# Differential attention of a hybrid decoder step: prompt scores of both components in two halves of the array's rows, component weights on GpSimd, a prompt step within the sample softmax, turned weights in other banks

## The chip, the cores and the metric

The kernel runs on one core of a Trainium2 chip. The engines are TensorE (PE: matmuls and transposes into PSUM; PEld are its weight loads), VectorE (DVE), ScalarE (ACT), GpSimd (POOL) and SyncE (SP, which issues most DMAs). The metric is the device time of one launch in microseconds (us), the median of several runs.

## The reference

One layer of a decoder serves a prompt of 512 rows and a sample group of 8 sequences of 4 rows with the same weights. The part that matters here is differential attention: 4 heads, each with two 64-wide components of q and k and a 128-wide v.

```python
def diff_attend(q, k, v, mask, lam):
    s = jnp.einsum('bqhcd,bkhcd->bhcqk', q.astype(jnp.float32), k.astype(jnp.float32)) * (DA_QK_DIM ** -0.5)
    s = jnp.where(mask[None, None, None], s, -jnp.inf)
    p = jax.nn.softmax(s, axis=-1)
    a = p[:, :, 0] - lam * p[:, :, 1]
    return jnp.einsum('bhqk,bkhd->bqhd', a, v.astype(jnp.float32))
```

The prompt is done in 4 blocks of 128 query rows; block b sees 128(b+1) keys. The sample rows see 256 cached keys and 4 new ones. Around it stand an mLSTM head group, an output projection, cross-attention into 256 memory tokens and a gated FFN with a short convolution.

## The kernel before

The program is one straight stream of about 17,000 instructions. A framework schedules it: the code emits operations, and the framework's own timing model decides the order in which each engine issues them, each engine then working through its own list in order. Python generators set what is emitted near what. Float32 matmuls run in two passes, so one `mm` of float32 operands is two rows of the trace; the matmuls of weights have operands split into high and low parts of a rounded float32 type and run in one pass each.

The stage that the change touches runs from about 246 to 302 us of the span. Two things are interleaved in it:

- **The prompt**: 16 groups i (block b = i // 4, head h = i % 4), run by `pipe(4 * H, da_soft, idle, da_turn, da_av, da_end)`. One `next(prompt)` is a step: it emits the scores and the softmax of group i, the transposes of group i - 2, the product with v of group i - 3, and after a block's last head its norm. `da_soft` takes two score banks `sda`, one for each component, from the pool `mm` (5 PSUM banks), multiplies 128 queries with 128(b+1) keys for each component, adds the causal mask to the last 128 columns by a bf16 matmul with the identity, takes row maxima on DVE, exponentials and row sums `su` on ACT, then the weights `rc` (reciprocals of the two sums, the second times the first sum and -lambda) and joins the components with them in `pda` on DVE. `da_turn` transposes `pda` into a bank `tpa`, ACT copies it to `aT`; `da_av` multiplies it with `dvN`.
- **The samples**: for each of 8 sequences `dk_load`, `dk_turn` (transposes `tpk` of cached keys) and `dk_scores` (`ssc`, four heads in four column quarters of the array). `sample_softmax` then makes weights `csz`, combines the components (`spa`), copies them (`spc`), transposes them (`spt`) and spreads them over `az`. Then come the products with the cached v (`ops`, four column quarters). In the first loop `next(prompt)` runs once per turn, ten times; the next five run beside the loads of v.

Both components of q lie in one tile `dqT` (and of k in `dkT`), component 0 in partitions 0 to 63, component 1 in 64 to 127. To multiply one component alone, the kernel keeps a second tile `dqz` with the lower half zeroed (four ACT copies and a POOL memset) and zeroes the upper half of `dqT` (four POOL memsets). Each score matmul so contracts over all 128 rows of the array, half of them zeros.

The pool `at` has 3 PSUM banks and serves transposes and small results (`tpk`, `mlt`, `dat`, `spa`, `spt`, `ops`). Tiles with the tag `S` share 11 buffers in SBUF; `dqz` takes one. Weights of the next projection (`w_out`) are loaded to staging buffers that the cached v occupies until `ops` has used it. After the stage the output projection runs, with the last groups' transposes and products among its matmuls.

Of the kernel before, what the change touches and what calls it, by code (L numbers as in the profile page):

```python
# [7 lines left out]
F32 = mybir.dt.float32  # L8
# [4 lines left out]
ALU = mybir.AluOpType  # L13
AX = mybir.AxisListType

P = 128
DM = 1024
SEQ = 512
NB = 8
# [3 lines left out]
H = 4  # L23
# [54 lines left out]
def kernel(ctx: ExitStack, tc: tile.TileContext, I, O):  # L78
    nc = tc.nc
    MUL, ADD, SUB, MAX, MIN = ALU.mult, ALU.add, ALU.subtract, ALU.max, ALU.min  # L80
# [9 lines left out]
    cst = ctx.enter_context(tc.tile_pool(name="cst", bufs=1))  # L90
# [11 lines left out]
    def S(shape, dt, name):  # L102
        return sp.tile(list(shape), dt, name=name, tag="S")
# [10 lines left out]
    def at(name="at"):  # L114
        return psa.tile([P, 512], F32, name=name, tag="at")

    def mmp(name="mm"):
        return psm.tile([P, 512], F32, name=name, tag="mm")
# [11 lines left out]
    mm = nc.tensor.matmul  # L130
# [24 lines left out]
    def con(n, p=P):  # L155
        o, w = CONST_COLS[n]
        return cpk[:p, o:o + w]
# [182 lines left out]
    @contextmanager  # L340
    def burst(ins):

        if ins is None:
            yield
        else:
            with tc.issue_after(ins), tc.high_priority():
                yield
# [687 lines left out]
        VRED(out=nm[:, b:b + 1], in_=ps, axis=AX.X, op=MAX, negate=True)  # L1035
        ACT(out=sall[:, b, :], in_=ps, func=AF.Exp, bias=nm[:, b:b + 1], accum_out=su[:, b:b + 1])

    def sample_softmax(sall, su, coef, sel, oname):


        cf = small(NB, "scf")
        nc.vector.reciprocal(out=cf, in_=su)
        if coef is not None:
            VTS(out=cf, in0=cf, scalar1=coef, scalar2=None, op0=MUL)
        VTT(out=cf, in0=cf, in1=sel, op=MUL)
        VTT(out=view(csz, 0, [(64, NB // 2), (48, 2), (1, 16)]),
            in0=con("comb").unsqueeze(1).unsqueeze(1).broadcast_to([P, NB // 2, 2, 16]),
            in1=cf.rearrange("p (i e) -> p i e", e=2).unsqueeze(3).broadcast_to([P, NB // 2, 2, 16]), op=MUL)
        az = S([P, 2, H, NB * NS], F32, oname + "z")
        nc.gpsimd.memset(az, 0.0)  # L1050
        w = sall.shape[2]
        pa = at("spa")
        for e in range(2):
            for i in range(NB // 2):
                mm(pa[NS * i:NS * i + NS, :w], lhsT=csz[:, 2 * i + e, :], rhs=sall[:, 2 * i + e, :], start=(e == 0), stop=(e == 1))
        a = Z("spc")[:, :w]
        nc.scalar.copy(out=a, in_=pa[:, :w])
        pT = at("spt")
        for g in range(2):
            tr(pT[:, g * P:(g + 1) * P], a[:, g * P:(g + 1) * P], ident)  # L1060
        for g in range(2):
            src = pT[:, g * 128:(g + 1) * 128].rearrange("p (b h t) -> p h b t", b=NB, h=H)
            for h in range(H):
                nc.scalar.copy(out=view(az, g * 1024 + h * 256, [(36, NB), (1, TS)]), in_=src[:, h])
        return a, [az[:, 0], az[:, 1]]
# [100 lines left out]
        rr = slice(64 * c, 64 * c + 64)  # L1166
        nc.gpsimd.tensor_copy(out=qz[rr, :, :, c, :], in_=dqT[rr, :, SEQ:].rearrange("p h (g r) -> p h g r", g=2))


    dqz = S([P, H, SEQ], F32, "dqz")  # L1170
    nc.gpsimd.memset(dqz[0:64], 0.0)
    for b in range(4):
        c = slice(b * P, b * P + P)
        nc.scalar.copy(out=dqz[64:128, :, c], in_=dqT[64:128, :, c])
        nc.gpsimd.memset(dqT[64:128, :, c], 0.0)

    kst, kts, pts, aTs, outs, rcs = {}, {}, {}, {}, {}, {}

    def dk_load(b):
# [22 lines left out]
    def da_soft(i):  # L1202
        b, h = i // H, i % H
        c0 = b * P
        nk = c0 + P
        pt = pts[i] = N("pda").rearrange("p (c k) -> p c k", c=2)
        nm = small(2, "nm")
        su = small(2, "su")
        sv = [mmp("sda")[:, :nk] for _ in range(2)]
        for c in range(2):  # L1210
            mm(sv[c], lhsT=(dqz if c else dqT)[:, h, c0:c0 + P], rhs=dkT[:, h, 0:nk], start=True, stop=False)
            mm(sv[c][:, c0:nk], lhsT=identb, rhs=cmaskb, start=False, stop=True)
        for c in range(2):
            VRED(out=nm[:, c:c + 1], in_=sv[c], axis=AX.X, op=MAX, negate=True)
            ACT(out=pt[:, c, :nk], in_=sv[c], func=AF.Exp, bias=nm[:, c:c + 1], accum_out=su[:, c:c + 1])
        rc = sm.tile([P, 2], F32, name="rc", tag="rc", bufs=6)
        nc.vector.reciprocal(out=rc, in_=su)
        VTS(out=rc[:, 1:2], in0=rc[:, 1:2], scalar1=su[:, 0:1], scalar2=nlam, op0=MUL, op1=MUL)
        STT(out=pt[:, 0, :nk], in0=pt[:, 1, :nk], scalar=rc[:, 1:2], in1=pt[:, 0, :nk], op0=MUL, op1=ADD)
        rcs[i] = rc  # L1220

    def da_turn(i):
        b = i // H
        nk = (b + 1) * P
        tp = mmp("tpa")
        for j in range(b + 1):
            tr(tp[:, j * P:(j + 1) * P], pts[i][:, 0, j * P:(j + 1) * P], ident)
        aTs[i] = Z("aT")
        nc.scalar.copy(out=aTs[i][:, :nk], in_=tp[:, :nk])
# [22 lines left out]
    for t, _ in enumerate(pipe(NB, dk_load, dk_turn, dk_scores)):  # L1252
        if t == 3:
            F.add(out_gate())
        F.run(2.5)
        next(prompt)
        F.run(2.5)
    aw, az = sample_softmax(sall, su, cv, con("selD"), "da")
    F.run(4)
    pz = Z("pz")[:, :NS]  # L1260
    VTT(out=v2(pz, TS), in0=aw[:, 256:260].unsqueeze(1).broadcast_to([P, NB, TS]),
# [616 lines left out]
```

## Time and profile before

| | |
|---|---|
| median of 3 runs | 960.0 us (959.2 to 962.14) |
| the profiled execution's own time | 957.37 us |
| its span | 955.6 us |
| instructions | 17087 |
| DVE busy | 600.3 us (63%) |
| ACT busy | 387.7 us (41%) |
| POOL busy | 196.4 us (21%) |
| PEclk | 0.9 or more in all slices but the last |

The span is the time from the first to the last instruction of the profiled execution; what lies around it is 957.37 - 955.6 = 1.8 us. A row of the timeline gives a start, a duration, the engine, the line, the operation, what it writes and reads and how many rows were merged; in square brackets stands the idle time before it and who ended it. Durations of matmuls are modelled and overlap, so what a matmul costs is read from the starts of neighbouring rows.

### The profile page before, as it was taken

Reading aid. Unit: us, or ns where it says so; the run is one execution under the profiler, and the core shown is the slowest. Engines: PE = TensorE matmul, PEld = TensorE weight load, DVE = VectorE, ACT = ScalarE, POOL = GpSimd, SP = SyncE. Lnnn points to the kernel's source line nnn. Section 1 sums busy time; section 2 is a strip of 40 time slices with the busy share of each in tenths; the row PEclk is TensorE's granted clock in tenths of the full one; section 3 lists DMA queues with packets and bytes.
Section 4 is the critical chain, followed back from the end, with each engine's and each line's share of the span. In section 5 each row is a group of like instructions: output and inputs, shape, how many; then the busy total and the mean of one; then the engine's idle time right before and its main releaser. Section 6 shows DMA issues by size and latency. Waiting matters only on the chain. (4 is left out here: it accounts for less than half of the span.)

```text
span 955.6 us, 17087 instructions
## 1 busy us (share of the span) xinstructions
PE 933.3 (98%) x6619; PEld 810.2 (85%) x6619; DVE 600.3 (63%) x1129; ACT 387.7 (41%) x750; POOL 196.4 (21%) x383
## 2 busy tenths in 40 slices
PE   8999999999999999999999999999999999999995
PEld 5899787889766778998767799989988997999974
DVE  6745145565886448635654769727758676676767
ACT  5655134344676357635544523332212222222232
POOL 6610000115432216300000454001110110110114
PEclk9999999999999999999999999999999999999998
DMA  8950023344825539946954743063053313512023
GB/s 296 296 178 1 1 88 136 88 131 137 275 82 171 173 100 346 289 137 188 344 195 115 206 133 88 4 177 89 4 144 82 119 26 81 162 48 89 24 92 116
DMA packets 120674, 130.27 MB, mean 136 GB/s; under 512 B 8568, under 2 KB 86233, under 8 KB 120593
## 3 DMA queue, kind: packets, MB, share of 16 engines
q1 hardware_dynamic: 114408, 125.69, 42.3%
q10 hardware_dynamic: 6184, 3.48, 1.2%
q8 instruction: 52, 0.85, 0.4%
q14 instruction: 30, 0.24, 0.1%
HBM read 112.22 MB, written 16.93 MB: 135 GB/s over the span
## 5 line engine op out<-in xcount | busy, mean ns | idle before, releaser
L146 ACT CAST wslot<-wst 128x1024 fp32r<-128x1024 f32 x125 | 130.8, 1050 | 261.3 <-issue 73.5
L477 PE MATMUL mm<-fT,wslot 128*128 128x256 f32 x1872 | 235.9, 288 | 0.0
L477 PEld LDWEIGHTS mm<-fT,wslot 128*128 128x128 f32 x1872 | 234.4, 188 | 1.8 <-issue 0.8
L147 DVE TENSOR_TENSOR wslot<-wst,wslot 128x1024 fp32r<-128x1024 f32 x125 | 154.4, 1238 | 91.8 <-ACT wslot L146 91.4
L1689 PE MATMUL mm<-wslot,act 128*128 128x512 f32 (+1 forms) x180 | 70.2, 391 | 0.0
L1690 PE MATMUL mm<-wslot,act 128*128 128x512 f32 (+1 forms) x180 | 70.0, 392 | 0.0
L1688 PE MATMUL mm<-wslot,act 128*128 128x512 f32 (+1 forms) x180 | 69.3, 387 | 0.0
L1596 POOL COPY cvo<-u 128x2 f32<-128x2 f32 x43 | 11.0, 256 | 204.7 <-DVE u L1594 194.6
L407 PE MATMUL mm<-wslot,hT 128*128 128x512 f32 x128 | 51.6, 403 | 0.0
L477 PE MATMUL mm<-hT,wslot 128*128 128x256 f32 (+1 forms) x384 | 51.0, 289 | 0.0
L409 PE MATMUL mm<-wslot,hT 128*128 128x512 f32 x128 | 51.0, 400 | 0.0
L408 PE MATMUL mm<-wslot,hT 128*128 128x512 f32 x128 | 50.7, 396 | 0.0
L1591 DVE TENSOR_TENSOR u<-mm,rsb 128x256 f32<-128x256 f32 x43 | 18.2, 424 | 51.0 <-PE mm L477 50.0
L477 PEld LDWEIGHTS mm<-hT,wslot 128*128 128x128 f32 x384 | 49.2, 188 | 0.5 <-issue 0.2
L1688 PEld LDWEIGHTS mm<-wslot,act 128*128 128x128 f32 x180 | 34.3, 191 | 8.0 <-issue 0.4
L1690 PEld LDWEIGHTS mm<-wslot,act 128*128 128x128 f32 x180 | 33.8, 188 | 7.2 <-issue 0.4
L1689 PEld LDWEIGHTS mm<-wslot,act 128*128 128x128 f32 x180 | 33.8, 188 | 7.2
L1608 ACT ACTIVATE c<-c 128x560 f32<-128x560 f32 x21 | 14.1, 672 | 56.5 <-DVE c L1602 56.5
L1602 DVE SCALAR_TENSOR_TENSOR c<-u,cvT,c 128x560 f32<-128x560 f32 x43 | 34.3, 798 | 0.9
L1601 DVE SCALAR_TENSOR_TENSOR c<-u,cvT,c 128x560 f32<-128x560 f32 x43 | 34.1, 793 | 0.2
L1701 DVE TENSOR_TENSOR yp<-mm,yp 128x512 f32<-128x512 f32 (+1 forms) x41 | 27.2, 674 | 5.1 <-PE mm L1690 5.0
L409 PEld LDWEIGHTS mm<-wslot,hT 128*128 128x128 f32 x128 | 24.1, 188 | 5.1
(474 smaller groups left out, 1863.8 us busy)
## 6 DMA issues: line engine op xcount, KB each, us to landing
wst<-in_w_up_dram SPq DMA_DIRECT2D x42, 512.0 KB
wst<-in_w_in_dram SPq DMA_DIRECT2D x28, 512.0 KB
wst<-in_w_down_dram SPq DMA_DIRECT2D x20, 512.0 KB
wst<-in_cache_mem_k_dram SPq DMA_DIRECT2D x16, 512.0 KB
wst<-in_w_mk_dram SPq DMA_DIRECT2D x8, 512.0 KB
xb<-in_x_prompt_dram SPq DMA_DIRECT2D x8, 512.0 KB
wst<-in_cache_dk_dram SPq DMA_DIRECT2D x16, 256.0 KB
wst<-in_cache_dv_dram SPq DMA_DIRECT2D x16, 256.0 KB
```

Of the source, the lines that this page charges most:

```text
L146: nc.scalar.copy(out=hi, in_=src)
L147: (eng or nc.vector).tensor_tensor(out=lo, in0=src, in1=f32(hi), op=SUB)
L407: mm(ps[b], lhsT=xt.hi(k, c0, c0 + n), rhs=s[:, 0, kk, :], start=(k == 0), stop=False)
L408: mm(ps[b], lhsT=xt.hi(k, c0, c0 + n), rhs=s[:, 1, kk, :], start=False, stop=False)
L409: return mm(ps[b], lhsT=xt.lo(k, c0, c0 + n), rhs=s[:, 0, kk, :], start=False, stop=(k == nk - 1))
L477: mm(ps[i], lhsT=s[:, l, k, :], rhs=x(k, c0, c1), start=(k == 0 and j == 0), stop=(k == 7 and j == 2))
L1601: STT(out=c, in0=u[:, 1:EXT - 1], scalar=w[1], in1=c, op0=MUL, op1=ADD)
L1602: STT(out=c, in0=u[:, 0:EXT - 2], scalar=w[0], in1=c, op0=MUL, op1=ADD)
L1688: mm(ps, lhsT=t[:, 0, c0:c0 + P], rhs=s[:, 0, i % 2, cs], start=st, stop=False)
L1689: mm(ps, lhsT=t[:, 0, c0:c0 + P], rhs=s[:, 1, i % 2, cs], start=False, stop=False)
L1690: return mm(ps, lhsT=t[:, 1, c0:c0 + P], rhs=s[:, 0, i % 2, cs], start=False, stop=en)
L1701: VTT(out=y, in0=ps, in1=y, op=ADD)
```

## The change

Four things change, all in the stage above.

1. `dqz` goes, with its copies and memsets. The two score matmuls of a group read partitions 0 to 63 and 64 to 127 of `dqT` and `dkT`, so that each uses one half of the array's rows, and write two banks as before. `burst(t)` asks the scheduler to issue the second right behind the first; the two mask matmuls come after both.
2. The weights `rc` are made on GpSimd: a power of -1 (`pow` with a tile `mone` of -1) in place of DVE's reciprocal, and the `tensor_scalar` behind it there too.
3. `sample_softmax` gets a hook `between`. The tenth `next(prompt)` no longer runs in the loop's last turn, but between the copy `spc` and the transposes `spt`.
4. `da_turn` takes its bank from `at` instead of `mm` for blocks 2 and 3.

```diff
-    def sample_softmax(sall, su, coef, sel, oname):
+    def sample_softmax(sall, su, coef, sel, oname, between=lambda: None):
...
         a = Z("spc")[:, :w]
         nc.scalar.copy(out=a, in_=pa[:, :w])
+        between()
         pT = at("spt")
...
-    dqz = S([P, H, SEQ], F32, "dqz")
-    nc.gpsimd.memset(dqz[0:64], 0.0)
-    for b in range(4):
-        c = slice(b * P, b * P + P)
-        nc.scalar.copy(out=dqz[64:128, :, c], in_=dqT[64:128, :, c])
-        nc.gpsimd.memset(dqT[64:128, :, c], 0.0)
-
+    mone = cst.tile([P, 2], F32, name="mone")
+    nc.gpsimd.memset(mone, -1.0)
...
+        t = None
         for c in range(2):
-            mm(sv[c], lhsT=(dqz if c else dqT)[:, h, c0:c0 + P], rhs=dkT[:, h, 0:nk], start=True, stop=False)
-            mm(sv[c][:, c0:nk], lhsT=identb, rhs=cmaskb, start=False, stop=True)
+            rr = slice(64 * c, 64 * c + 64)
+            with burst(t):
+                t = mm(sv[c], lhsT=dqT[rr, h, c0:c0 + P], rhs=dkT[rr, h, 0:nk], start=True, stop=False).ins
+        with tc.issue_after(t):
+            for c in range(2):
+                mm(sv[c][:, c0:nk], lhsT=identb, rhs=cmaskb, start=False, stop=True)
...
-        nc.vector.reciprocal(out=rc, in_=su)
-        VTS(out=rc[:, 1:2], in0=rc[:, 1:2], scalar1=su[:, 0:1], scalar2=nlam, op0=MUL, op1=MUL)
+        GTT(out=rc, in0=su, in1=mone, op=ALU.pow)
+        nc.gpsimd.tensor_scalar(out=rc[:, 1:2], in0=rc[:, 1:2], scalar1=su[:, 0:1], scalar2=nlam, op0=MUL, op1=MUL)
...
-        tp = mmp("tpa")
+        tp = (at if b > 1 else mmp)("tpa")
...
-        next(prompt)
+        if t < NB + 1:
+            next(prompt)
         F.run(2.5)
-    aw, az = sample_softmax(sall, su, cv, con("selD"), "da")
+    aw, az = sample_softmax(sall, su, cv, con("selD"), "da", lambda: next(prompt))
```

How the engines' lists change is shown at three places. The first is on PE, at a group of block 2 (i = 9), right ahead of the sample softmax. `sda` are the score banks, `cb` the identity and mask, `oda` the product with v. Before:

```order
L1237 MATMUL oda<-dvN,aT 128x128 x2
L1227 MATMUL tpa<-cpk,pda 128x128 x2
L1211 MATMUL sda<-dkT,dqT 128x384
L1212 LDWEIGHTS cb
L1212 MATMUL sda<-cb 128x128
L1211 MATMUL sda<-dkT,dqz 128x384
L1212 LDWEIGHTS cb
L1212 MATMUL sda<-cb 128x128
```

After the change:

```order
L1238 MATMUL oda<-dvN,aT 128x128 x2
L1228 MATMUL tpa<-cpk,pda 128x128 x2
L1210 MATMUL sda<-dkT,dqT 128x384 x2
L1213 LDWEIGHTS cb
L1213 MATMUL sda<-cb 128x128
L1213 LDWEIGHTS cb
L1213 MATMUL sda<-cb 128x128
```

The two score matmuls now stand next to each other, and both masks behind them. This holds for 15 of the 16 groups; in the group i = 3 four transposes `tpk` stand between the two.

The second place is on PE too, right behind the first: the sample softmax, with the last of the cached-key scores (`ssc`, sequence 7) ahead of it after the change. Before, the score rows on top are those of i = 10:

```order
L1211 MATMUL sda<-dkT,dqz 128x384
L1212 LDWEIGHTS cb
L1212 MATMUL sda<-cb 128x128
L1055 MATMUL spa<-das,csz 32x260 x8
L1060 MATMUL spt<-cpk,spc 128x128 x2
L1264 MATMUL npn<-cpk,pz 32x128
```

After the change:

```order
L1192 MATMUL ssc<-kT,qz 32x260 x4
L1238 MATMUL oda<-dvN,aT 128x128 x2
L1228 MATMUL tpa<-cpk,pda 128x128 x2
L1210 MATMUL sda<-dkT,dqT 128x384 x2
L1213 LDWEIGHTS cb
L1213 MATMUL sda<-cb 128x128
L1213 LDWEIGHTS cb
L1213 MATMUL sda<-cb 128x128
L1055 MATMUL spa<-das,csz 32x260 x8
L1061 MATMUL spt<-cpk,spc 128x128 x2
L1266 MATMUL npn<-cpk,pz 32x128
```

The scores on top are now those of i = 9: one prompt step fewer stands ahead of `spa`, and one more behind `npn`. Nothing stands between `spa` and `spt`, as before.

The third place is on POOL, where the gated mLSTM rows are written to `mixT` (in the before code between copies to `kT`), early in the stage. After the change the weights `rc` of the groups 2 and 3 stand among them (L1218 the power, L1219 the product):

```order
L147 TENSOR_TENSOR mixT_2775<-mltm,mixT_2774 128x4x128
L1182 COPY kT<-dkT 128x4x4
L147 TENSOR_TENSOR mixT_2775<-mltm,mixT_2774 128x4x128 x2
L1218 TENSOR_TENSOR rc<-su,mone 128x2
L147 TENSOR_TENSOR mixT_2775<-mltm,mixT_2774 128x4x128
L147 TENSOR_TENSOR mixT_2775<-mltm,mixT_2774 128x4x32
L1182 COPY kT<-dkT 128x4x4
L1219 TENSOR_SCALAR rc<-rc,su,nlam 128x1
L1218 TENSOR_TENSOR rc<-su,mone 128x2
L1219 TENSOR_SCALAR rc<-rc,su,nlam 128x1
```

So three writes to `mixT` stand ahead of the power of group 2, and two more between it and its product.

## The prediction

> **What bounds the kernel now.** I read the busy times of the page first, then busy time in stretches of 5 us, then PE's timeline with its waits.
>
> ```profile
> PE 933.3 (98%) x6619; PEld 810.2 (85%) x6619; DVE 600.3 (63%) x1129; ACT 387.7 (41%) x750; POOL 196.4 (21%) x383
> ```
>
> PE is the bound of the whole, so a microsecond taken from PE's list is worth a microsecond wherever PE doesn't stand waiting. In the stage that is changed (246 to 302 us) this has to be looked at again, since other engines come close there. The columns are the stretch, its length, then busy time and instructions of PE, PEld, DVE, ACT and POOL, the clock, and DMA:
>
> ```profile
> 250.00:255.00 5.00, 4.93 (x45) 3.91 (x45) 4.83 (x17) 3.74 (x16) 1.16 (x3) 1.00 0.99 336
> 255.00:260.00 5.00, 4.25 (x40) 3.33 (x39) 4.96 (x15) 5.00 (x19) 4.87 (x6) 1.00 0.96 323
> 285.00:290.00 5.00, 5.00 (x74) 3.40 (x73) 3.02 (x6) 2.58 (x8) 1.28 (x1) 1.00 0.86 258
> ```
>
> Up to 260 us DVE and ACT are full, and from 285 us on only PE is. PE's timeline shows three waits of over half a microsecond in the stage:
>
> ```profile
> 258.56 0.30 PE L1227 MATMUL tpa<-cpk,pda 128*128 128x128 f32 x1 [0.75 <-DVE pda L1219]
> ...
> 268.17 0.41 PE L1227 MATMUL tpa<-cpk,pda 128*128 128x128 f32 x2 [0.63 <-ACT pda L1215]
> ...
> 280.71 0.44 PE L1060 MATMUL spt<-cpk,spc 128*128 128x128 f32 x2 [0.70 <-ACT spc L1057]
> ```
>
> Two, together 1.4 us, are for the softmax of a prompt group (`pda`), both in blocks 0 and 1; one, 0.7 us, is for the copy ahead of `spt`. So the stage is PE's list plus about 2 us.
>
> **Term 1, the scores.** What a score matmul costs is read from the distance of its start to its mask's. One group of each block, and behind the first and last what follows:
>
> ```profile
> 254.72 0.39 PE L1211 MATMUL sda<-dkT,dqT 128*128 128x128 f32 x2
> 254.94 0.22 PE L1212 MATMUL sda<-cb 128*128 128x128 bf16 x1
> ...
> 268.42 0.60 PE L1211 MATMUL sda<-dkT,dqT 128*128 128x256 f32 x2
> 268.85 0.22 PE L1212 MATMUL sda<-cb 128*128 128x128 bf16 x1
> ...
> 269.54 0.65 PE L1197 MATMUL ssc<-kT,qz 128*32 128x260 f32 x8
> 270.12 0.71 PE L1237 MATMUL oda<-dvN,aT 128*128 128x128 f32 x4
> 270.67 0.60 PE L1081 MATMUL dat<-cpk,dasq 128*128 128x128 f32 x4
> ...
> 282.19 0.81 PE L1211 MATMUL sda<-dkT,dqT 128*128 128x384 f32 x2
> 282.84 0.22 PE L1212 MATMUL sda<-cb 128*128 128x128 bf16 x1
> ...
> 287.21 1.02 PE L1211 MATMUL sda<-dkT,dqT 128*128 128x512 f32 x2
> 288.07 0.22 PE L1212 MATMUL sda<-cb 128*128 128x128 bf16 x1
> 288.13 1.08 PE L1211 MATMUL sda<-dkT,dqz 128*128 128x512 f32 x2
> 289.04 0.22 PE L1212 MATMUL sda<-cb 128*128 128x128 bf16 x1
> 289.19 1.08 PE L1279 MATMUL ops<-wst,daz 128*32 128x128 f32 x32
> ```
>
> The two passes take 0.22, 0.43, 0.65 and 0.86 us for 128, 256, 384 and 512 keys. If the second component's matmul runs in the other half of the rows at the same time, one of the two is saved in each group: 4 heads x (0.22 + 0.43 + 0.65 + 0.86) = 8.6 us. The group i = 3 has four transposes between its two, so 0.2 us of it is lost: **-8.4 us**. No matmul of this trace uses 64 of the rows, so the overlap has to be judged by its neighbour, four column quarters:
>
> ```profile
> 328.56 1.93 PE L386 MATMUL mm<-wst,xts 128*32 128x256 f32 x32
> 330.42 0.95 PE L407 MATMUL mm<-wslot,mixT 128*128 128x512 f32 x3
> ```
>
> 32 passes of 256 columns take 1.86 us; one after the other, at 0.43 / 2 each, they would take 6.9 us. So four run at once, across both passes. The bounds are no overlap (0) and full overlap (-8.4); I take full, the nearest row's answer.
>
> **Term 2, changing the array's division.** A mask followed by a full matmul takes 0.06 us (288.07 to 288.13), one followed by column quarters 0.15 (289.04 to 289.19): 0.09 us to go in. `ssc` (260 columns, two passes, 0.44 us by the row of 256) takes 0.58 us to the next full matmul: 0.14 to come out. The row halves go in and out once a group, twice for i = 3: 17 x 0.23 = **+3.9 us** (bounds 0, if the drain hides, and 3.9). The masks cost what they did. So PE's list gets 4.5 us shorter: nothing from the 128-key groups (0.22 against 0.23), 2.5 us from the 512-key ones, in the stretch where only PE is full.
>
> The Trainium skill speaks against the full saving: its page "TensorE: Matmul & The Clock Gate", Part 3, measured 3.07 times the speed, not 4, for four row tiles. By that share (0.77) two halves would be 1.53 times as fast, and Term 1 an estimated -5.8 us; no run here shows it.
>
> **Term 3, the step within the softmax.** What the code moves is not what PE's list shows: between `spa` and `spt` there stands nothing, so the 0.7 us wait stays. But `spa` now comes one prompt step earlier behind the last `ssc`, and its weights `csz` have their own chain:
>
> ```profile
> 273.75 0.65 PE L1197 MATMUL ssc<-kT,qz 128*32 128x260 f32 x8
> ...
> 278.93 1.09 PE L1055 MATMUL spa<-das,csz 128*32 128x260 f32 x16
> ```
>
> ```profile
> 276.96 0.56 DVE L1214 TENSOR_REDUCE nm<-sda 128x1 f32<-128x384 f32 x1
> ...
> 277.63 0.29 DVE L1046 TENSOR_TENSOR csz<-cpk,scf 128x128 f32<-128x128 f32 x1
> ```
>
> From the last `ssc` to the end of `csz` passed 4.2 us, with two row maxima of the prompt between; PE had 5.2 us of other work. After the change PE has `ssc` 0.58, `oda` 0.55 (270.12 to 270.67), two transposes of one pass (0.22), a pair of 384 keys with going in and out (0.88) and two masks (0.06 + 0.15): 2.4 us. The chain, with one maximum (0.56) less, takes 3.6. PE waits **+1.2 us** for `csz` (0 if PE waited ahead of it already, 1.8 with the old chain). The step itself isn't lost; it runs behind.
>
> **Term 4, the weights on GpSimd.** DVE sheds a reciprocal and a product in each group, POOL takes a power and a product:
>
> ```profile
> L1217 DVE RECIPROCAL rc<-su 128x2 f32<-128x2 f32 x15 | 2.4, 159 | 2.6 <-ACT pda L1215 2.5
> L1218 DVE TENSOR_SCALAR rc<-rc,su,nlam 128x1 f32<-128x1 f32 x14 | 3.8, 270 | 0.2
> ...
> L304 POOL TENSOR_TENSOR dars<-dars,mhalf 128x4 f32<-128x4 f32 x4 | 5.6, 1408 | 0.3
> L304 POOL TENSOR_TENSOR rs<-rs,mhalf 128x1 f32<-128x1 f32 x1 | 0.5, 548 | 0.1
> L302 POOL TENSOR_SCALAR rs<-ssq 128x1 f32<-128x1 f32 x1 | 0.2, 191 | 13.3 <-ACT dasq L309 13.3
> L147 POOL TENSOR_TENSOR mixT<-mltm,mixT 128x512 fp32r<-128x512 f32 x4 | 5.1, 1295 | 0.9 <-ACT mixT L146 0.8
> ```
>
> DVE loses 16 x 0.43 = 6.9 us. A power on two columns isn't in the trace: between 0.55 (one) and 1.41 (four), 0.84 by the line through both; with a product of 0.2 to 0.3 it makes 1.1 us against DVE's 0.43. Each group's chain so gets 0.7 us longer, while DVE, full up to 260 us, gets to it sooner. Bounds: the 1.4 us of waits for `pda` go (-1.4), or each of the eight groups up to block 1, where steps are shortest, waits half of the 0.7 (+3). I take the waits halved, **-0.7 us**, since DVE was full where they fell. The other bank of `tpa` I set to nothing, since it changes blocks 2 and 3, where PE's list shows no wait at `tpa`; the vanished copies of `dqz` too, since they lie ahead of the stage, where PE was full of projections (bounds 0 and, for a stall that they had hidden, the 0.7 us of one such wait).
>
> **The sum.** -8.4 + 3.9 + 1.2 - 0.7 = -4.0 us. The profiled execution took 957.37 us (span 955.6 and 1.8 around it), so it becomes 953.4; the median of the runs shown lies 2.6 above it, so I forecast **956.0 us**. Behind the stage PE's lists are as before, and PE is busy 98% of the whole span, so I let the gain be carried to the end. About 0.3% (2.9 us) is what a measurement of this kernel can tell from no change.
>
> **The rivals.**
>
> - *No waits are left at `pda`*: DVE's 6.9 us end them all, and bring `csz` in time: -8.4 + 3.9 - 1.4 = -5.9, so 960.0 - 5.9 = 954.1 us. For it: DVE was at 4.83 and 4.96 of 5 us up to 260 us. Chance 0.12.
> - *The chain takes the place of PE*: with shorter steps, two steps no longer cover scores, maxima, exponentials and the slower weights: -8.4 + 3.9 + 1.2 + 3 = -0.3, 959.7 us. For it: PE already waited for `pda` at two steps. Against: from 285 us on, v's products stand between. Chance 0.24.
> - *Half an overlap*: the second pass of one half waits for the first pass of the other, so three pass times remain of four: -4.2 + 3.9 + 1.2 - 0.7 = +0.2, 960.2 us. Against: column quarters show no such thing. The Trainium skill's 3.07 above stands between this and the forecast: with its Term 1 the sum would be an estimated -1.4 us. Chance, for any such part, 0.08.
> - *The halves don't overlap at all* and only the going in and out remains: +3.9 + 1.2 - 0.7 = +4.4, 964.4 us. Chance 0.06.
> - *Slower, by POOL's list*: POOL works in order, and long operations stand ahead of the weights. Three writes to `mixT` (1.3 each) stand ahead of group 2's; the norms of blocks 0 to 2 (0.19 + 1.41 and a product) and a memset ahead of others. With five such bursts of 2.8 us and a slack of 1.4 us in the chain (an estimate, halfway between 0 and the burst) PE waits 5 x 1.4 = 7.0 us: -8.4 + 3.9 + 1.2 + 7.0 = +3.7, 963.7 us. It decides for slower than before once the slack is under about 2.1 us. Against: the transposes come two steps after the scores. Chance 0.08.
>
> A port speaks for this last one. A join of 128 columns took 1.37 us while POOL ran, where another took 0.34:
>
> ```profile
> 257.04 1.37 DVE L1219 SCALAR_TENSOR_TENSOR pda<-pda,rc 128x128 f32<-128x128 f32 x1
> ...
> 261.11 0.34 DVE L1219 SCALAR_TENSOR_TENSOR pda<-pda,rc 128x128 f32<-128x128 f32 x1
> ```
>
> ```profile
> 256.99 2.97 POOL L147 TENSOR_TENSOR mixT<-mltm,mixT 128x512 fp32r<-128x512 f32 x3
> ```
>
> The Trainium skill's page "SBUF — State Buffer", section "Who interferes with whom", says that a DVE instruction with two SBUF inputs and a GpSimd instruction that reads SBUF exclude each other; the trace agrees with these rows.
>
> **How the numbers follow.** The forecast (-2.5 to -5) has 0.42. Faster by over 0.3%: 0.37 of it and the first rival's 0.12, 0.49. Slower by over 0.3%: the last two rivals and a tail, 0.15. The rest, 0.36, is within. The range takes in the forecast, the first rival with room below, the chain and the half overlap with the spread of the runs above: 952.5 to 961.5 us; about 0.2 is left out.
>
> **What would show it.** Term 1: scores of both components starting within a few hundredths, and about 0.9 us to the first mask for 512 keys; 1.3 us refutes it by half, 1.7 wholly. Term 2: 0.09 us more from a mask to the next scores. Term 3: a wait of `spa` for `csz` near 1.2 us, and `spt` still waiting 0.7. Term 4: L1218 near 0.84 us, and PE's waits for `pda` under 1.4 us; several waits of 1 us or more at `tpa` mean the chain or POOL's list. If the stage keeps its 57 us with fewer busy PE, the sum was wrong in Term 4; if it shrinks and the total doesn't, the loss lies behind it.

## The result, and the profile after

The changed kernel takes 966.9 us (median of 6 runs, 965.56 to 968.45), the kernel before beside it 958.86 (957.02 to 962.14): a ratio of 1.0082, 95% interval 1.0066 to 1.0098. It is 8 us slower; the forecast was 956.0 us, faster, and the range ended at 961.5. The profiled execution took 966.51 us (span 964.7).

The page's busy times, first line, and below it the windows that answer to those shown of before (stretch, length, busy time and instructions of PE, PEld, DVE, ACT and POOL, granted clock, DMA), with one more of the stage's last third:

```profile
PE 939.3 (97%) x6619; PEld 812.1 (84%) x6619; DVE 595.6 (62%) x1097; ACT 387.3 (40%) x748; POOL 208.8 (22%) x411
...
250.00:255.00 5.00, 4.04 (x36) 2.88 (x34) 3.54 (x10) 3.73 (x13) 2.18 (x5) 1.00 0.78 252
255.00:260.00 5.00, 5.00 (x46) 3.53 (x48) 4.83 (x14) 4.74 (x16) 3.98 (x5) 1.00 1.07 371
285.00:290.00 5.00, 5.00 (x46) 3.25 (x46) 2.45 (x5) 3.28 (x15) 1.43 (x3) 0.71 0.01 4
295.00:300.00 5.00, 3.18 (x36) 1.52 (x34) 1.37 (x2) 1.71 (x4) 0.32 (x1) 1.00 0.94 318
```

PE's busy time did not fall, it rose by 6 us, and two things are new: a stretch (285 to 290) in which PE is full but its clock is 0.71, and one (295 to 300) in which no engine is full and PE stands 1.8 us. PE's timeline of the changed kernel has these waits in the stage (idle time and its releaser in brackets):

```profile
251.69 0.66 PE L1186 MATMUL tpk<-cpk,wst 128*128 128x128 f32 x4 [0.96 <-ACT kT L1187]
...
278.31 0.65 PE L1192 MATMUL ssc<-kT,qz 128*32 128x260 f32 x8 [1.42 <-DVE kT L1187]
...
282.68 1.09 PE L1055 MATMUL spa<-das,csz 128*32 128x260 f32 x16 [1.80 <-DVE csz L1046]
284.28 0.57 PE L1061 MATMUL spt<-cpk,spc 128*128 128x128 f32 x2 [0.51 <-ACT spc L1057]
...
300.03 0.94 PE L1238 MATMUL oda<-dvN,aT 128*128 128x128 f32 x6 [1.84 <-ACT aT L1230]
...
309.24 1.16 PE L1238 MATMUL oda<-dvN,aT 128*128 128x128 f32 x8 [0.57 <-ACT aT L1230]
```

With two small ones (0.22 and 0.28) they come to 7.6 us, against 2.6 before. And behind the longest of them the clock falls. PE alone by the microsecond (stretch, length, busy time and instructions, clock, DMA):

```profile
281.00:282.00 1.00, 0.00 (x0) 1.00 0.00 0
...
284.00:285.00 1.00, 0.72 (x4) 0.72 0.00 0
285.00:286.00 1.00, 1.00 (x7) 0.50 0.06 16
286.00:287.00 1.00, 1.00 (x5) 0.50 0.00 0
287.00:288.00 1.00, 1.00 (x5) 0.57 0.00 0
...
299.00:300.00 1.00, 0.00 (x0) 1.00 1.04 401
...
301.00:302.00 1.00, 1.00 (x4) 0.75 0.99 373
302.00:303.00 1.00, 1.00 (x12) 0.50 0.31 117
...
307.00:308.00 1.00, 1.00 (x6) 0.50 0.00 0
308.00:309.00 1.00, 0.67 (x5) 0.83 0.00 0
```

The missing shares of 284 to 288 add up to 1.7 us, those of 301 to 309 to 3.4: 5.1 us of PE's time lost to half clock in the stage, where before it was 1.00 throughout. So the stage, from the first score matmul to the one behind the last mask, can be split into idle time, half clock and the rest, PE's work at full clock:

| | stage | idle | half clock | work |
|---|---|---|---|---|
| before | 56.8 us (245.7 to 302.5) | 2.8 | 0 | 54.0 |
| after | 63.9 us (247.6 to 311.5) | 7.7 | 5.1 | 51.1 |

Half clock counts half of the time that PE was busy at a clock of 0.50. The stage is 7.1 us longer: 3.0 less work, 4.9 more idle, 5.1 at half clock. Of the 9.1 us between the two profiled executions 2.0 lie ahead of the stage. There the changed kernel has half clock for 6.8 us from 8 us on and for 3.4 us at 97 us, the kernel before for 3.4 us at 8 us alone. Such stretches come at these two places in the profiles of other arrangements too, and are missing in others.

### The profile page after: what moved, and what is told of

It is laid out like the page before. It is cut to its first block, busy times and chain, and to the rows that moved or that the text cites. A ratio compares the mean times of both kernels' runs of the same rounds, so it can differ in the third digit from the quotient of the medians.

```text
span 964.7 us, 17096 instructions
## 1 busy us (share of the span) xinstructions
PE 939.3 (97%) x6619; PEld 812.1 (84%) x6619; DVE 595.6 (62%) x1097; ACT 387.3 (40%) x748; POOL 208.8 (22%) x411
## 5 line engine op out<-in xcount | busy, mean ns | idle before, releaser
L304 POOL TENSOR_TENSOR rs<-ssy,mhalf 128x1 f32<-128x1 f32 (+1 forms) x10 | 6.5, 647 | 105.7 <-DVE ssy L1130 102.8
```

## The experiments

My first theory, from the waits above, was that two of the parts did it: the step (1.80 us at `spa`) and the banks of `tpa` (the casts of `w_out` ahead of `aT`), each with half clock behind. The rivals were the longer chain through GpSimd, and the row halves themselves. Every edit makes the scheduler plan anew, so a run shows an edit with the order that comes of it.

A comparison always has the kernel before on the same chip; the ratio is to it. The columns from "profiled" on are of one profiled execution each: its own time, then the stage split as above (us). It can lie some 4 us from the median: the one of no_step was the slowest of its executions, those of pair_order, rows_only, block3_casts, before_casts and change_held the fastest. The last column counts the groups with row halves in which no other matmul stands between the two halves in PE's list.

| kernel | median | ratio, 95% interval | profiled | stage | idle | half clock | work | halves together |
|---|---|---|---|---|---|---|---|---|
| the change | 966.9 | 1.0082 (1.0066 to 1.0098) | 966.5 | 63.9 | 7.7 | 5.1 | 51.1 | 15 of 16 |
| no_bank | 968.2 | 1.0097 (1.0077 to 1.0118) | 967.1 | 67.4 | 7.8 | 4.5 | 55.1 | 12 of 16 |
| no_step | 963.5 | 1.0046 (1.0029 to 1.0064) | 967.4 | 64.5 | 7.6 | 4.4 | 52.5 | 15 of 16 |
| no_pool | 967.6 | 1.0094 (1.0074 to 1.0115) | 968.8 | 68.2 | 6.1 | 9.0 | 53.0 | 13 of 16 |
| rows_only | 965.7 | 1.0082 (1.0068 to 1.0097) | 964.8 | 63.4 | 7.2 | 1.7 | 54.4 | 12 of 16 |
| no_rows | 965.2 | 1.0074 (1.0061 to 1.0087) | 967.1 | 62.5 | 7.6 | 0 | 54.9 | none used |
| pair_order | 962.5 | 1.0064 (1.0041 to 1.0088) | 960.9 | 60.6 | 5.6 | 0 | 55.0 | none used |
| rows_block3 | 961.8 | 1.0041 (1.0025 to 1.0058) | 959.9 | 60.1 | 5.2 | 1.1 | 53.8 | 2 of 4 |
| filled_wait | 964.8 | 1.0073 (1.0060 to 1.0086) | 965.0 | 64.4 | 7.5 | 4.5 | 52.5 | 15 of 16 |
| block3_casts | 958.8 | 1.0004 (0.9994 to 1.0014) | 955.9 | 57.1 | 3.9 | 0 | 53.1 | 2 of 4 |
| rows_casts | 962.3 | 1.0043 (1.0027 to 1.0060) | 961.6 | 59.2 | 5.7 | 0 | 53.5 | 12 of 16 |
| before_casts | 964.0 | 1.0068 (1.0055 to 1.0081) | 959.8 | 56.0 | 2.4 | 0 | 53.6 | none used |
| before_held | 957.1 | 0.9985 (0.9976 to 0.9995) | 957.8 | 56.6 | 2.5 | 0 | 54.1 | none used |
| block3_held | 958.1 | 0.9998 (0.9988 to 1.0009) | 957.1 | 57.8 | 3.0 | 1.7 | 53.1 | 2 of 4 |
| change_held | 964.0 | 1.0061 (1.0043 to 1.0078) | 961.1 | 61.5 | 8.1 | 1.7 | 51.7 | 15 of 16 |

### Undoing one part at a time

**no_bank** takes the fourth part back:

```diff
-        tp = (at if b > 1 else mmp)("tpa")
+        tp = mmp("tpa")
```

> The change without its fourth part: tpa keeps its banks in the pool mm in all blocks. In the changed kernel ACT works off three casts of w_out ahead of the exponentials of group 12 and stands 4.3 us for the first one's load; PE then waits 1.84 and 0.57 us for aT, and the granted clock stands at 0.50 for two stretches of 3.4 us. With the old banks only one cast stands ahead of group 12. Theory 1 (the banks moved the casts, and the idle PE lost the clock): the waits for aT fall under 0.5 us together, no stretch at 0.50 behind 300 us, about 2 + 3.4 us less than the 966.9 of the change, 961.5 us (959.5 to 963). Theory 2 (the casts only stand there because the whole sample chain is late, banks play no part): ACT still stands for w_out, 965 us or more.

It stayed at 1.0097. The 1.84 us for `aT` did go, but a wait of 2.49 us at `tpa` came in their place, and the half clock with it. Theory 1 on the banks falls. In the new arrangement PE's list also has `ops` between the halves of three more groups (11 to 13), and the work is 4.0 us more than the change's.

**no_step** lets the tenth prompt step run in the loop again:

```diff
-        if t < NB + 1:
-            next(prompt)
+        next(prompt)
...
-    aw, az = sample_softmax(sall, su, cv, con("selD"), "da", lambda: next(prompt))
+    aw, az = sample_softmax(sall, su, cv, con("selD"), "da")
```

> The change without its third part: the tenth prompt step runs in the loop again, so spa stands behind the scores of group 10. Theory 1 (the step took away the cover of the chain to csz: 1.80 us of wait at spa and one stretch of 3.4 us at half clock, but the late w_out casts come of the banks): the wait at spa falls under 0.5 us and the stretch at 0.50 ahead of 288 us is gone, the one behind 300 us stays; 966.9 - 1.8 - 1.7 = 963.4 us (961.5 to 965). Theory 2 (all that is late comes from the late sample chain): the wait for w_out goes with it, 959 us or less.

The wait at `spa` fell to 0.45 us and no half clock stood ahead of 288 us; 963.5 us is what theory 1 had. The two intervals don't overlap; the third part so costs some 3 us, with the arrangement that comes of it. In the profiled execution idle time stayed at 7.6: behind 300 us a wait of 2.37 us for `aT` and three stretches at half clock stand. But this was the slowest of the six, at a mean clock of 0.983, where the other five had 0.990 to 0.996.

**no_pool** makes the weights on DVE again:

```diff
-        GTT(out=rc, in0=su, in1=mone, op=ALU.pow)
-        nc.gpsimd.tensor_scalar(out=rc[:, 1:2], in0=rc[:, 1:2], scalar1=su[:, 0:1], scalar2=nlam, op0=MUL, op1=MUL)
+        nc.vector.reciprocal(out=rc, in_=su)
+        VTS(out=rc[:, 1:2], in0=rc[:, 1:2], scalar1=su[:, 0:1], scalar2=nlam, op0=MUL, op1=MUL)
```

> The change without its second part: the weights rc are made on DVE by a reciprocal and a product again. If the longer chain through GpSimd (0.70 + 0.34 us a group against 0.43, and waits behind POOL's other work) is what the stage lost, most waits at tpa, tpk and aT go, and it is 962 us or less. If the loss comes of the banks and the step (its order on ACT still has two to three w_out casts ahead of group 12, and spa behind group 9), it stays within 2 us of 966.9, with DVE 7 us busier.

1.0094: the loss isn't GpSimd's alone. The 1.42 us for `kT` went, `spa` waits 2.08 instead, and the clock was at half from 298 to 315 us.

**rows_only** makes these three edits together, so that only the row halves are left of the change (`dqz` gone, both halves, then both masks):

> The first part alone: the two score matmuls in two halves of the array's rows, dqz gone; weights on DVE, step in the loop, tpa in mm as before. If the row halves bring what the sum gave them (-8.4 for the overlap, +3.9 for going in and out, and back some 1.4 for three groups of which the second half starts late) and all the loss lies in the other three parts: 958.9 - 3 = 955.8 us (954 to 957.5), PE's idle time in the stage no more than before's 2.6 us. If the row halves themselves cost it (two banks of the five are taken at once and read behind one another), waits for sda's readers show on PE and it is 959 us or more.

965.7 us, as slow as the whole change. But its work is 54.4 us, no less than the 54.0 before: in four groups (3, 4, 13 and 14) other matmuls stand between the halves, and in three more (6, 7 and 9) the second half starts up to 0.3 us late. So this kernel shows what its arrangement costs, not what row halves are worth where they overlap. And **no_rows** undoes the row halves alone (`dqz` back, each mask behind its scores), the other three parts kept:

> The change without its first part: full-array scores with dqz, mask behind each, but weights on GpSimd, step within the softmax and tpa banks as changed. If the row halves are what costs the time, it is near before: 958.9 us (957 to 961), idle PE in the stage (first score to last mask) about before's 2.8 us. If the other three parts cost as much by themselves (spa behind group 9, three w_out casts ahead of group 12 on ACT), idle is 5 us or more, with stretches at half clock, and it is 963 us or more.

965.2 us. So, as arranged here, either half of the change costs all of it, and the costs don't add up. That speaks for one thing in the stage with little slack, which every part touches; it doesn't prove it, since each arrangement is a new one.

### The order alone, and the place

**pair_order** is the kernel before, full-array scores and `dqz`, with nothing but the changed order of a group's four matmuls:

```diff
+        t = None
         for c in range(2):
-            mm(sv[c], lhsT=(dqz if c else dqT)[:, h, c0:c0 + P], rhs=dkT[:, h, 0:nk], start=True, stop=False)
-            mm(sv[c][:, c0:nk], lhsT=identb, rhs=cmaskb, start=False, stop=True)
+            with burst(t):
+                t = mm(sv[c], lhsT=(dqz if c else dqT)[:, h, c0:c0 + P], rhs=dkT[:, h, 0:nk], start=True, stop=False).ins
+        with tc.issue_after(t):
+            for c in range(2):
+                mm(sv[c][:, c0:nk], lhsT=identb, rhs=cmaskb, start=False, stop=True)
```

> The kernel before (full-array scores, dqz, all else as before) with the changed order alone: both score matmuls of a group next to each other, then both masks. The work of PE is that of before. If the arrangement starves PE (two banks taken at once, both row maxima late and back to back), idle PE in the stage rises from 2.8 to 5 us or more and it is 962 us or more. If the waits come only because PE's part of each group got shorter than the chain behind it, idle stays under 4 us and it is 958.9 us, within 1.5.

1.0064, with 1 us more work for PE and 2.8 us more idle time: the arrangement by itself costs. Where, DVE's timeline of this kernel shows; the row maxima (`nm`) of two groups and the norm's sum `dass` stand between the steps of `scf` and `csz`:

```profile
277.65 0.20 DVE L1042 RECIPROCAL scf<-ssu 128x8 f32<-128x8 f32 x1
277.76 0.97 DVE L1218 TENSOR_REDUCE nm<-sda 128x1 f32<-128x384 f32 x2
278.65 0.22 DVE L1044 TENSOR_SCALAR scf<-scf,cv 128x8 f32<-128x8 f32 x1
279.01 0.69 DVE L1076 TENSOR_REDUCE dass<-dasq 128x4 f32<-128x512 f32 x1
279.62 0.15 DVE L1045 TENSOR_TENSOR scf<-scf,cpk 128x8 f32<-128x8 f32 x1
279.78 1.02 DVE L1218 TENSOR_REDUCE nm<-sda 128x1 f32<-128x384 f32 x2
280.72 0.28 DVE L1046 TENSOR_TENSOR csz<-cpk,scf 128x128 f32<-128x128 f32 x1
```

From the reciprocal to the end of `csz` pass 3.35 us. Before, the reciprocal stood here, with two maxima between it and `csz`, and `dass` behind:

```profile
276.30 0.20 DVE L1042 RECIPROCAL scf<-ssu 128x8 f32<-128x8 f32 x1
...
279.61 0.68 DVE L1076 TENSOR_REDUCE dass<-dasq 128x4 f32<-128x512 f32 x1
```

To the end of `csz` (277.63 + 0.29) it was 1.6 us. After the change in order PE waits 1.26 us for `csz`, and 1.75 us at the stage's end:

```profile
281.06 1.09 PE L1055 MATMUL spa<-das,csz 128*32 128x260 f32 x16 [1.26 <-DVE csz L1046]
...
304.54 0.66 PE L1231 MATMUL tpa<-cpk,pda 128*128 128x128 f32 x4 [1.75 <-DVE pda L1223]
```

**rows_block3** has the row halves only for 512 keys; `dqz` serves blocks 0 to 2:

```diff
+        if b in (3,):
+            t = None
+            for c in range(2):
+                rr = slice(64 * c, 64 * c + 64)
...
+        else:
+            for c in range(2):
+                mm(sv[c], lhsT=(dqz if c else dqT)[:, h, c0:c0 + P], rhs=dkT[:, h, 0:nk], start=True, stop=False)
...
```

> Row halves in block 3 alone (512 keys), where PE was the only full engine; blocks 0 to 2, the weights, the step and the banks as before. A 512-key group took 1.98 us from its first score to behind its second mask and takes 1.28, with 0.09 to go in: 4 x 0.6 = 2.4 us less work. If the waits of the change come from blocks 0 to 2, where maxima, exponentials and csz are late, the gain stays: 956.5 us (955 to 958). If a chain off PE (loads of w_out, casts, exponentials) sets the end of this stretch, the gain turns into idle PE: 958.9 us or more, with over 2 us more idle behind 285 us.

961.8 us, slower than before, although nothing ahead of 285 us moved (PE idle as before up to there). Most of the gain was never there: of the 2.4 us less work 0.2 shows (53.8 against 54.0). `burst` asks the scheduler and doesn't force it, and in the groups 13 and 14 matmuls of `ops` stand between the halves:

```profile
289.79 1.12 PE L1215 MATMUL sda<-dkT,dqT 64*128 64x512 f32 x2
290.85 0.65 PE L1289 MATMUL ops<-wst,daz 128*32 128x128 f32 x16
291.42 1.12 PE L1215 MATMUL sda<-dkT,dqT 64*128 64x512 f32 x2
292.48 0.28 PE L1218 MATMUL sda<-cb 128*128 128x128 bf16 x2
```

Each half alone takes 1.06 us, together 2.1, where the two full-array products took 0.86 and 0.91 (287.21 to 288.07 and 288.13 to 289.04 before). So only two of the four groups overlap. The rest of the loss, 2.4 us more idle and 1.1 at half clock, stands behind 285 us, on ACT's list:

```profile
292.06 1.05 ACT L146 CAST wslot<-wst 128x1024 fp32r<-128x1024 f32 x1 [2.91 <-DMA wst<-in_w_out_dram]
```

The load of `w_out` can't start before `ops` has freed the cached v's buffers. The program put this cast ahead of an exponential of group 12; ACT stands 2.91 us for the load, PE then 0.91 us for `aT` and 1.65 us at `tpa`. In the changed kernel it is 4.33 us, ahead of both exponentials and of the copy that PE's 1.84 us is for:

```profile
298.30 1.04 ACT L146 CAST wslot<-wst 128x1024 fp32r<-128x1024 f32 x1 [4.33 <-DMA wst<-in_w_out_dram]
299.25 0.36 ACT L1240 ACTIVATE dao<-oda,rc 128x128 f32<-128x128 f32 x1
299.51 0.47 ACT L1230 COPY aT<-tpa 128x384 f32<-128x384 f32 x1
```

The second chain of the stage so runs from the cached keys through `ssc`, `csz`, `spa` and `ops` to the load of `w_out` and its casts. Its times, from the starts of these rows (for `csz` its end), counted from the first score matmul (us):

| | last `ssc` | `csz` ready | `spa` | first `w_out` cast | first projection matmul |
|---|---|---|---|---|---|
| before | 28.4 | 32.3 | 33.3 | 46.3 | 56.9 |
| pair_order | 28.3 | 34.8 | 34.8 | 48.1 | 60.6 |
| rows_block3 | 28.1 | 32.0 | 33.0 | 47.2 | 60.1 |
| rows_only | 29.1 | 35.3 | 35.3 | 49.0 | 63.4 |
| the change | 31.0 | 34.9 | 35.1 | 50.7 | 63.9 |

No version here has this chain earlier in a way that counts (0.3 us at `csz` in rows_block3), and the change has it 1.8 us later at `spa` and 4.4 us later at the cast.

### Taking the casts out of the way

**block3_casts**, **rows_casts** and **before_casts** make the high halves of the first four `w_out` slots on GpSimd:

```diff
+        if share == 2:
+            nc.gpsimd.tensor_copy(out=sv[:, 0], in_=st)
+            VTT(out=sv[:, 1], in0=st, in1=f32(sv[:, 0]), op=SUB)
+            return
...
-        slotsA(w_out, n0)
+        slotsA(w_out, n0, share=2 if n0 in (0,) else False)
```

> Row halves in block 3 alone, and besides the casts of the first four w_out slots on GpSimd instead of ACT (POOL does next to nothing there), so that neither the exponentials nor the copies aT stand behind a cast that waits for its load. With the casts on ACT this kernel had PE idle 0.91 us for aT and 1.65 us at tpa, and 1.1 us went to half clock. Theory 1 (PE's gain came back as waits because ACT's list stands for w_out): those go, 961.8 - 3.7 = 958.1 us (956.5 to 959.5). Theory 2 (the chain of maximum, exponential and join of 512 keys is itself longer than PE's shortened steps): the waits at tpa and aT stay, 961 us or more.

> Row halves in all blocks (the first part alone), with the casts of the first four w_out slots on GpSimd. Theory 1: of its waits those behind 290 us go (1.32 us for a score bank, 0.95 and 0.42 behind it) and the stretch at half clock (1.7 us), those at csz (1.33 + 0.50 + 0.85) stay: 965.7 - 4.4 = 961.3 us (960 to 963). Theory 2: as without, 965 us or more.

> The kernel before with the casts of the first four w_out slots on GpSimd alone. ACT stood 2.3 us for w_out there too, but PE lost 0.22 us by it: 958.3 us, within 1.2, by theory 1. If it is faster by over 2 us, ACT's list held the kernel before as well; if it is slower by over 2 us, the moved casts cost something of their own, and the two kernels beside it have to be read against this one.

With row halves the casts' removal brought 3.0 us (961.8 to 958.8) and 3.4 us (965.7 to 962.3), near theory 1's 3.7 and 4.4, and the half clock behind 290 us went. But the control became slower, by 5.5 us (964.0 against 958.5): its stage is 0.8 us shorter, but behind it PE waits 2.30 us at `tpa` and 0.81 for `dasq`. So these two gains prove less than they seem to. Read against this control, row halves in block 3 are 5.2 us faster, but in the stage their work is only 0.5 us less (53.1 against 53.6); the difference is the control's loss behind the stage.

**before_held**, **block3_held** and **change_held** leave the casts on ACT and let each be issued only behind the exponentials of a given group:

```diff
+            with tc.issue_after(exps[share[0]]):
+                nc.scalar.copy(out=sv[:, 0], in_=st)
...
-        slotsA(w_out, n0)
+    for k, g in zip(range(0, 8, 2), (12, 13, 13, 14)):
+        slotA(w_out, k, 0, share=(g,))
```

> Control: the kernel before with the first four casts of w_out on ACT held behind the exponentials of the groups 12, 13, 13 and 14. ACT's order changes at two places only. PE lost 0.22 us by these casts before, so either theory has 958.5 us, within 1.

> Row halves in block 3 alone, with the same hold. Theory 1 (ACT's list standing for the load of w_out gave the gain back): the 0.91 and 1.65 us of idle PE and the 1.1 us of half clock of the kernel without the hold go, and 2.4 us less work remains: 957.5 us (956 to 959), below the control. Theory 2 (the chain of 512 keys through maximum, exponential, join is longer than PE's shortened steps): a wait of over 1 us at tpa stays, 960 us or more.

> The changed kernel with the same hold: one cast behind group 12's exponentials instead of three ahead of them. Theory 1: the waits for aT (1.84 and 0.57 us) and the two stretches at half clock behind 300 us (3.4 us) go, the waits ahead of 290 us stay: 966.9 - 5.8 = 961.1 us (959.5 to 963). Theory 2: the chain is late anyway and the wait moves to the first matmuls of the projection or to tpa: 965 us or more.

This control hardly moves: 957.1 us, 0.15% (0.05 to 0.24) faster than before, and the only kernel here whose interval lies below 1. Row halves in block 3 go from 961.8 to 958.1 with the hold, and the two waits shrink to one:

```profile
299.23 2.07 PE L1254 MATMUL oda<-dvN,aT 128*128 128x128 f32 x8 [0.52 <-ACT aT L1246]
```

So theory 1 holds for the waits, but not for its time: the row halves should then have beaten the control, and stand at 958.1 against 957.1. Its profiled execution has only 1.1 us less work than the control's, in place of 2.4, because again two of its four groups have `ops` between the halves; against that stand 0.5 us more idle and one stretch at half clock, 1.7 us. The changed kernel, in which 15 pairs stay together, gains 2 (by the ratios) to 2.9 us (by the medians) of the expected 5.8, and the two intervals overlap: the half clock behind 300 us is gone, but two held casts, now done without waiting, stand ahead of an `aT`, and PE still waits 2.59 us.

### The clock

**filled_wait** puts three matmuls that nothing reads into the wait ahead of `spa`; the order of the other work is the same but for one place on DVE:

```diff
         pa = at("spa")
+        for _ in range(3 if oname == "da" else 0):
+            mm(pa[:, 0:256], lhsT=ident, rhs=sall[:, 7, 0:256], start=True, stop=True)
```

> The changed kernel with three matmuls that compute nothing used (identity times exponentials, float32, 256 columns, 0.43 us each, 1.3 us) on PE ahead of spa, where it waited 1.80 us for csz; spa overwrites them; all else in the same order. If idle PE costs the clock (every stretch of 3.41 us at half clock followed one with PE busy 2.2 us or less), the stretch from 281.0 to 284.4 has 2.5 us of busy PE in place of 1.25, and no half clock follows it: 966.9 - 1.7 = 965.2 us. If half clock comes from something else, it stands there as before, and the time stays at 966.9 or goes up.

At this place the clock stayed up. PE of this kernel, where the change had 0.72, 0.50 and 0.50:

```profile
281.00:282.00 1.00, 0.60 (x7) 1.00 0.00 0
...
284.00:285.00 1.00, 1.00 (x10) 1.00 0.00 0
285.00:286.00 1.00, 1.00 (x10) 1.00 0.00 0
286.00:287.00 1.00, 1.00 (x27) 1.00 0.00 0
```

The time, 964.8 us, is near the 965.2 expected, but its ratio (1.0073) can't be told from the change's (1.0082). At the stage's end `aT` was late by 3.04 us in this profile, with three stretches at half clock. That idle PE costs the clock at this place is supported by the other profiles too: no_bank, no_pool and change_held, with the same kind of wait and PE busy 1.43 to 1.58 us in the 3.41 us there, drop to half clock behind it as the change does (1.25); filled_wait (2.46) and no_step (2.56) don't. What it is worth in the median isn't shown.

## Why the prediction was wrong

**What failed first is the sentence that the stage is PE's list plus about 2 us.** It was read from PE's waits before, which were short. But a short wait doesn't tell how far the next bound is. Beside PE's list runs the samples' chain to the load of `w_out`, and it had little slack: before, `csz` was ready 1.0 us ahead of `spa`, and ACT already stood 2.3 us for `w_out`. With PE's work 3.0 us less, idle rose by 4.9 us. pair_order shows that the order of four matmuls alone, with the same matmuls, makes `csz` 2.5 us late. In no_rows, with the other three parts alone, it is 1.2 us late and idle 4.8 us more. The windows that the prediction looked at leave out 260 to 285 us, where `csz` is made; DVE was busy 3.1 to 4.7 and ACT 3.6 to 4.3 of each 5 us there, so neither had much room. That this chain is the whole reason stays in part argued: every test of it came with a new arrangement.

**Term 1 and 2 (-8.4 and +3.9, together -4.5) measured -3.0**, of which 0.4 are four transposes that only moved behind the stage, so 1.9 us are missing. The overlap is as forecast where both halves start together. Pairs of 256 and 512 keys, and a pair of 256 whose second half came late:

```profile
263.65 0.70 PE L1210 MATMUL sda<-dkT,dqT 64*128 64x256 f32 x4
264.29 0.28 PE L1213 MATMUL sda<-cb 128*128 128x128 bf16 x2
...
265.69 1.15 PE L1210 MATMUL sda<-dkT,dqT 64*128 64x256 f32 x4
266.77 0.28 PE L1213 MATMUL sda<-cb 128*128 128x128 bf16 x2
...
295.43 1.13 PE L1210 MATMUL sda<-dkT,dqT 64*128 64x512 f32 x4
296.50 0.29 PE L1213 MATMUL sda<-cb 128*128 128x128 bf16 x2
```

0.64 and 1.07 us to the first mask, where one component alone took 0.43 and 0.86: both for the price of one and 0.21, near the 0.23 of term 2. The second pair took 1.08. It is one of three whose second half came late, 0.4 to 0.5 us more each and 1.4 together; PE's weight loads waited there for ACT's exponentials, which free the score banks. In the group i = 3 nothing overlaps: 0.83 us in place of 0.42, where the sum had 0.2 of loss. Two banks at once, out of five, was not in the sum.

**Term 3 (+1.2 for `csz`, 0.7 stays at `spt`) measured 1.80 and 0.51.** The mechanism is right, and no_step confirms it (0.45 us with the step in the loop). The size is short by 0.6: on DVE a step of `scf` took 0.88 us, where it took 0.22 in pair_order above, and ended with a memset on POOL:

```profile
280.79 0.88 DVE L1044 TENSOR_SCALAR scf<-scf,cv 128x8 f32<-128x8 f32 x1
...
279.84 1.80 POOL L1050 MEMSET daz<- 128x2048 f32 x1
```

The memset stands behind the power of group 8 (from 277.94) and a write to `mixT` in POOL's list; in pair_order, without the weights there, it had ended at 276.78. The Trainium skill's page "SBUF — State Buffer", section "Who interferes with whom", counts `tensor_scalar` among the DVE operations that can take the port pair shared with GpSimd; these rows agree, with the step ending 0.03 us behind the memset.

**Term 4 (-0.7)**: the waits of `tpa` for `pda` (1.4 us) did go. The power took 0.70 us and the product 0.34, 1.04 against the forecast 1.1:

```profile
266.18 0.71 POOL L1218 TENSOR_TENSOR rc<-su,mone 128x2 f32<-128x2 f32 x1 [0.73 <-ACT pda L1216]
266.99 0.34 POOL L1219 TENSOR_SCALAR rc<-rc,su,nlam 128x1 f32<-128x1 f32 x1
```

But their place was taken by waits that the term didn't look at, for `kT` of the cached keys (0.96 and 1.42 us). Ahead of the second copy (on DVE) stand two maxima, a join and a step of the norm. The first (on ACT) stood behind a table load of 1.28 us and an exponential before as well and ends 4.0 us behind the first score matmul, where it was 4.7; but PE now comes to it sooner, with four transposes that need it ahead of `ssc`. no_pool has no 1.42, so that one hangs on the GpSimd weights; the 0.96 stays in it and in rows_only and is missing in no_rows, so it comes with the row halves.

**The edits set to nothing**: the other bank for `tpa` is worth nothing that can be measured (no_bank 1.0097 against 1.0082), as forecast, though no_bank also lost three overlaps, so the part wasn't alone.

**Not in the sum at all: the clock, 5.1 us.** In the trace before, the granted clock was 1.00 in the whole stage, and I took it as given. It is a price on idle time: two waits of 1.8 us were followed by 1.7 and 3.4 us lost. But 5.1 us is one execution. Over its six executions the changed kernel's mean granted clock was 0.984 to 0.992, and the two at the ends both took 966.5 us, though the profiled one (0.984) lost 0.008 of its span, 7.7 us, more to the clock. So half clock and waits can stand for each other, and how much of the 8 us the clock makes stays open. That it isn't all of it, no_rows shows, at 1.0074 without any half clock in its profiled stage.

**The rivals**: the chain that takes the place of PE (0.24, 959.7 us) was the right kind; its +3 us of waits were too few, and the half clock was missing. Nearest in time were the halves that don't overlap (964.4), which the rows of both halves starting together rule out, and POOL's list (963.7). no_pool, as slow with the weights on DVE, speaks against the last one as the cause, though POOL's list had its share: the memset that made `csz` late, and the 1.42 us.

What stays open: how the scheduler comes to place the casts and `dass` where it does, and so whether an order exists in which the row halves in all blocks win. None of the kernels run here had it: rows_only and rows_casts overlap only 12 of their 16 groups, and those with row halves in block 3 two of four.

## What to carry to other kernels

Before a saving on the bound engine is booked, follow the second chain of the stage from its first load to what the next stage waits for, and put a number on its slack: the saving counts only up to there. Where a scheduler places the work, run the new order with the old work once (as pair_order does), since it is a change of its own. Look in each new list whether what the saving needs is still there: here a pair that other matmuls part costs more than the two full products it replaces. And a wait of well over a microsecond on PE is priced above its length, since the clock may fall behind it.

## What the runs showed of the hardware

**Half clock comes in stretches of 3.41 us.** Their starts lie whole multiples of 3.41 us apart in a profile (284.44 and 301.51 in the changed kernel, 5 x 3.41). With the 16 profiles cut into these windows from 240 to 320 us, half clock followed all seven windows in which PE was busy 0.66 to 1.63 us, five of the 16 with 1.68 to 2.22 us, and one of the 333 with more (3.02 us, in block3_held). The Trainium skill's page "TensorE: Matmul & The Clock Gate", Part 1, has the half rate after about one idle window of 3.4 us; the stretches' length agrees, but here PE needed to be idle for no more than about half of one. It is no sharp rule: no_rows had windows with 1.87, 1.93 and 2.10 us busy and no drop, and the drop at 97 us of the changed kernel, also against the rule that filled_wait's expectation gives, followed a PE that was busy throughout by its records, though for 1.9 us of the 3.4 with matmuls of 4 and 8 columns.

**Two row halves run at the same time**, the second starting 7 ns behind the first in the trace's single rows. Each pass of a pair costs about 0.1 us more than a full-array pass of the same columns (0.21 for the two passes, at 256 as at 512 columns), and so does each pass of a half that runs alone (1.06 us for 512 columns in rows_block3). So two components of 512 keys took 1.07 us instead of 1.72, and two of 128 keys 0.42 (248.70 to 249.12) instead of 0.44.
